# Neighbourhood attention in a diffusion trunk: full-depth score products, a zero-padded half key tile, and a moved value projection

## The chip, the cores and the metric

The kernel runs on one core of one Trainium2 chip. The metric is the device time of one execution in microseconds (us), from three timed runs; lower is better. All arithmetic is in 32-bit floats. Where a product needs accuracy, its operands are split into a high part and a low remainder in a rounded 32-bit format (`F32R`), and two or three products are summed.

## The reference, cut to what matters

The program is one step of a two-layer trunk with 1024 sample tokens (a grid of 16 rows by 64 columns) and 128 prompt tokens. The change lies in the second layer, in mixer C, the neighbourhood attention with 8 heads of 64 channels. Each query reads all 128 context keys and a window of 8 grid rows by 16 columns, in one softmax, with a learned relative bias on the window part:

```
kn = k[:, idx_b];  vn = v[:, idx_b]                  # the 8 x 16 window of each query
s_nb = einsum('bqhd,bqnhd->bhqn', qblk, kn) * scale + rpb[:, dr_b, dc_b]
s_cx = einsum('bqhd,blhd->bhql', qblk, k_ctx) * scale
p = softmax(concatenate([s_cx, s_nb], axis=-1), axis=-1)
out = einsum('bhql,blhd->bqhd', p[..., :L], v_ctx) + einsum('bhqn,bqnhd->bqhd', p[..., L:], vn)
```

The 128 prompt tokens attend among themselves only. q, k, v and a gate come from one input projection of the layer's normalised tokens.

## The kernel before, in words

**Heads in pairs.** `layer1` (L1626) runs four pairs of heads, one `NeighborPair` each. A pair's queries, keys, values and gates are projected channel-major by `Proj.atoms` (L1330): for each of three token groups of 384 columns, eight channel tiles of three products each, into a PSUM bank `cg`. One *atom* is two channel tiles, that is six products of 128x384; one projection is 12 atoms.

**How rows are used.** The pair has 128 channels, 64 per head. `k_split` (L1376) makes for each head h a tile `KH[h]` whose 64 own rows hold the high part of the keys and whose other 64 rows hold a copy of it; ACT writes the high part, DVE subtracts to get the low part, and POOL or DVE copies the high part into the other rows. `q_evac` (L1447) makes `QP[h]`: high part of the scaled queries in head h's rows, low part in the other 64. So one product of 128 rows, `QP[h]` with `KH[h]`, gives high times high plus low times high. The third term, high queries with low keys, is a second product on 64 rows only, with one shared tile `KL` whose rows 0 to 63 belong to head 0 and 64 to 127 to head 1.

**One head, one tile of 128 queries.** `st1` (L1484) makes the scores into two PSUM banks `a`, `b` of a ring of three (tile name `cS`). The queries of tiles 2 to 5 (interior) see 9 grid rows, 576 columns of keys; tiles 0, 1, 6, 7 (edge) see 512; both see 128 context keys; tile 8 is the prompt. The keys are cut in pieces of 512 columns, the 64 left over (interior only) and the 128 of the context; every piece has a full-depth product and a 64-row product (L1506 to L1509). DVE then adds the bias table and takes the running maximum in two instructions (`ttr`, L1517 and L1518) and negates it (`cnm`, L1521); ACT takes the exponential with the row sums (L1522). The bias tables `E` (edge) and `Z` (interior, with 128 zero columns behind) are loaded by `bias` (L1354), masked on POOL by `mask` (L1365). For the edge tiles the context's zeros are the broadcast tile `kn.zero`.

`st2` (L1528) transposes the probabilities on PE in tiles of 128 keys (`cT`) and copies them to `PT` in SBUF, four tiles by ACT, the rest by DVE; the interior's last tile has 64 keys only, so 64 rows. `st3` (L1544) multiplies them with the values for both heads (`cpv`, each head in 64 columns of the array), with 64 rows for the half tile. `norm` (L1555) divides by the sums: `n0` multiplies the gate with `cpv` and takes reciprocals, `n1` spreads them with two half-width products per query tile (`cR`).

**Order.** The order of every engine's queue is written out by hand, as lists of atoms with an assumed cost. `attend` (L1580) lists for the 18 (tile, head) steps n: the scores of n, the transposes of n-2, and on every second step the values of n-4 and n-3. What comes after the last scores is returned apart, as the tail. `weave(main, fill, frac)` (L26) spreads the atoms of `fill` over the first `frac` of `main`; `merge` interleaves two lists. In `layer1` (L1676 to L1703), while pair n attends, the fill is: the last part of its own keys (`last_k`), then the gate, query and value projections of the next pair m, 12 atoms each. After that comes `m.k_start`, and the key projection of m (two token groups, 8 atoms) with the tail of n, the loads and masks of m's bias tables and its SiLU woven in. The fourth pair has as fill `last_k` and two gate projections of the next mixer.

**Memory.** SBUF tiles come from two rings of equal slots, S (25) and W (17). 16 S slots hold the layer's tokens. A weight chunk is loaded (`raw`, SP queue), its high part cast by ACT (`whi`) and its low part subtracted on POOL (`wlo`); `pre` does this for the chunk after the running one.

## Time and profile before

| | |
|---|---|
| three timed runs | 1690.11 us median, 1689.85 to 1690.24 |
| span of the profiled execution, first to last instruction | 1689.1 us; its own time is not recorded apart from this, so the medians' 1.0 us more is what lies around the span |
| instructions | 23950 |
| granted TensorE clock, mean | 0.979 (1.00 in every stretch of the neighbourhood attention) |
| score products of the four pairs, first and last start | 728.2 and 1117.2 us |
| DMA | 105.35 MB, mean 62 GB/s |

In the page, "busy" of PE is the union of modelled, overlapping matmul times, so a busy PE is no sign of a full one: what one product costs is the time from its start to the start of the next. A row of the timeline gives start (us from the span's start), duration (us), engine, line, operation, output<-inputs, array rows*columns and shape (rows x moving columns), count, and in brackets the idle time before it with what ended it. Where line 97 or 106 stands, a helper recorded the instruction, and the tile's name tells the step.

### The profile page before, as it was taken

To read this page: it belongs to the slowest core of one execution; us is meant where nothing else is said; L and a number is where in the kernel's file an instruction comes from. 1 tells how busy PE (TensorE), PEld (TensorE's weight loads), DVE (VectorE), ACT (ScalarE), POOL (GpSimd) and SP (SyncE) were. 2 spreads that over 40 slices of the span, in tenths; PEclk is the share of its full clock that TensorE was granted. 3 is DMA by queue.
4 is the path that set the end of the run, shared out by engine and by line. 5 is a ranking of instruction groups with operands and counts; after the bars stand their busy time and mean duration, and the time that the engine had idled before them with its cause. 6 is when DMAs were issued, how large, how long until landed. Compare 5 with 4: busy or idle time off the path is not lost.

```text
span 1689.1 us, 23950 instructions
## 1 busy us (share of the span) xinstructions
PE 1610.8 (95%) x9268; PEld 1247.9 (74%) x9268; DVE 851.8 (50%) x1839; ACT 647.3 (38%) x1358; POOL 606.3 (36%) x470
## 2 busy tenths in 40 slices
PE   5989999999899999999999999999999999999998
PEld 4968997945554788888888888889975566555686
DVE  3674232467776545524433444324575575766633
ACT  4331211355455323443433434325444343434311
POOL 1642221078567326421310313010135454547421
PEclk7999999999999999999999999999999999999999
DMA  9353013210001222211312113023000000012341
GB/s 305 114 189 88 26 38 131 84 48 14 0 14 50 88 94 73 62 41 34 60 29 51 42 35 58 15 72 96 1 18 19 14 26 14 20 31 82 129 139 50
DMA packets 118806, 105.35 MB, mean 62 GB/s; under 512 B 45924, under 2 KB 104548, under 8 KB 118692
## 3 DMA queue, kind: packets, MB, share of 16 engines
q1 hardware_dynamic: 118692, 103.81, 20.8%
q8 instruction: 73, 1.20, 0.3%
q14 instruction: 41, 0.34, 0.1%
HBM read 88.05 MB, written 15.75 MB: 61 GB/s over the span
## 4 chain that ended last, share of the span: by engine, by line
PE 81%; DVE 7%; ACT 2%; POOL 2%; issue 1%; DMA 0%; SPq 0%; DVEq 0%; POOLq 0%; ACTq 0%
PE cg L97 16%; PE yps L97 10%; PE st L97 9%; PE gate L97 8%; PE pv L97 7%; PE cS L97 6%; PE mp L97 5%; PE lat L97 4%; PE cpv L97 3%; PE cT L106 2%; PE dq L97 2%; PE qkv L97 1%; DVE ms L131 1%; DVE mx L933 1%; PE dk L97 1%
## 5 line engine op out<-in xcount | busy, mean ns | idle before, releaser
L124 POOL TENSOR_TENSOR acc<-acc,P 128x1024 f32<-128x1024 f32 x98 | 233.2, 2380 | 111.1 <-ACT P L969 106.7
L969 ACT ACTIVATE P<-st 128x512 f32<-128x512 f32 x288 | 167.5, 597 | 192.1 <-PE st L97 171.4
L933 DVE TENSOR_REDUCE mx<-mp 128x1 f32<-128x384 f32 x384 | 193.4, 550 | 93.3 <-PE mp L97 90.8
L124 POOL TENSOR_TENSOR wlo<-raw,whi 128x1024 fp32r<-128x1024 f32 x36 | 87.2, 2424 | 270.0 <-ACT whi L113 152.5
L97 PE MATMUL yps<-whi,ohl 128*128 128x512 f32 x576 | 183.4, 393 | 0.0
L97 PE MATMUL cg<-hT1h,whi 128*128 128x384 f32 x480 | 178.0, 371 | 1.8 <-DVE hf L133 1.2
L97 PE MATMUL cg<-hT1h,wlo 128*128 128x384 f32 x480 | 161.8, 337 | 1.8 <-POOL wlo L124 1.8
L97 PE MATMUL cg<-hT1l,whi 128*128 128x384 f32 x480 | 161.6, 337 | 0.0
L97 PEld LDWEIGHTS yps<-whi,ohl 128*128 128x128 f32 x576 | 108.1, 188 | 26.2 <-issue 2.4
L1522 ACT ACTIVATE cs<-cs,cnm 128x640 f32<-128x640 f32 (+1 forms) x64 | 54.9, 857 | 153.3 <-DVE cnm L131 153.0
L97 PE MATMUL yps<-wlo,ohl 128*128 128x512 f32 x288 | 112.2, 389 | 0.0
L97 PE MATMUL gate<-hTh,whi 128*128 128x384 f32 x288 | 100.5, 349 | 5.0 <-ACT whi L113 5.0
L97 PEld LDWEIGHTS cg<-hT1h,whi 128*128 128x128 f32 x480 | 90.3, 188 | 14.5 <-issue 7.0
L97 PE MATMUL gate<-hTh,wlo 128*128 128x384 f32 x288 | 99.2, 344 | 0.9 <-DVE wlo L121 0.9
L97 PE MATMUL gate<-hTl,whi 128*128 128x384 f32 x288 | 98.8, 343 | 0.0
L97 PEld LDWEIGHTS cg<-hT1h,wlo 128*128 128x128 f32 x480 | 90.1, 188 | 2.2 <-POOL wlo L124 2.2
L97 PEld LDWEIGHTS cg<-hT1l,whi 128*128 128x128 f32 x480 | 90.5, 189 | 0.0
L97 PE MATMUL pv<-P,dV 128*64 128x512 f32 x288 | 80.9, 642 | 0.0
L97 PE MATMUL pv<-P,V 128*64 128x512 f32 x288 | 78.6, 624 | 0.0
L113 ACT CAST whi<-raw 128x1024 fp32r<-128x1024 f32 (+2 forms) x60 | 61.8, 1038 | 18.8 <-DMA raw<-in_w_in_o 9.6
L124 POOL TENSOR_TENSOR acc<-P 128x1024 f32<-128x1024 f32 x14 | 33.3, 2380 | 92.9 <-ACT P L969 92.4
L97 PE MATMUL mp<-dKh,QH 96*128 96x384 f32 x192 | 61.2, 374 | 4.1 <-DVE mx L933 2.9
(412 smaller groups left out, 3581.7 us busy)
## 6 DMA issues: line engine op xcount, KB each, us to landing
raw<-in_w_in_o SPq DMA_DIRECT2D x20, 512.0 KB, 4.0
raw<-in_w_in_e SPq DMA_DIRECT2D x18, 512.0 KB, 7.0
wmb<-in_w_mod SPq DMA_DIRECT2D x16, 512.0 KB, 9.0
wm<-in_w_mod SPq DMA_DIRECT2D x16, 512.0 KB, 5.4
wg<-in_w_mod SPq DMA_DIRECT2D x16, 512.0 KB, 3.8
x<-xr SPq DMA_DIRECT2D x9, 512.0 KB, 2.6
xr<-x SPq DMA_DIRECT2D x9, 512.0 KB, 3.9
xn<-in_x_sample SPq DMA_DIRECT2D x8, 512.0 KB, 8.1
```

The costliest lines, as they stand in the source:

```text
L97: self.nc.tensor.matmul(out=out, lhsT=l, rhs=r, start=st, stop=sp)
L106: self.nc.tensor.transpose(out, in_, self.ident[0:n, 0:n])
L113: self.nc.scalar.copy(out=out, in_=in_)
L124: self.nc.gpsimd.tensor_tensor(out=out, in0=a, in1=b, op=op)
L131: self.nc.vector.tensor_scalar(out=out, in0=a, scalar1=s1, scalar2=None, op0=op0)
L933: kn.nc.vector.tensor_reduce(out=self.mx[:, h, t, c:c + 1], in_=b, axis=AX.X, op=ALU.max)
L969: kn.nc.scalar.activation(out=P[:, h], in_=a, func=AF.Exp, scale=self.scale)
L1522: nc.scalar.activation(out=s[:, 0:n], in_=s[:, 0:n], func=AF.Exp, bias=nm, accum_out=sm)
```

## The change

1. **Low keys on 128 rows.** Each head gets its own low-key tiles `KL[h]`, `KLp[h]`; the other head's 64 rows are set to zero once by POOL. They are shared by the four pairs (`NeighborShared`, made at the start of `layer1`). Every score product, high and low, now has 128 rows.
2. **Two key pieces.** The first piece is the 128 context keys together with the first 128 window keys, read as two segments of one access pattern (`seg2`); the second is the rest of the window, 448 columns (interior) or 384 (edge). The scores' columns, the bias tables (128 zero columns now in front, for both tables) and the transposed tiles follow this order; `kn.zero` goes.
3. **Half key tile padded.** The three `PT` buffers are fixed tiles whose slot 5 has zeros in rows 64 to 127, and the values' product of the half tile runs over 128 rows.
4. **Division.** `n0` also has ACT spread the reciprocals to a 128-column tile `crw` (from the W ring), and `n1` uses one full-width product per query tile instead of two half-width ones.
5. **Order.** The value projection of the next pair leaves the fill of the attention and stands ahead of the key projection behind the last scores; `k_start` comes after it; the tail, the bias loads, SiLU and then the masks are spread over the first 0.6 of both. The buffer `kx` is single instead of double.

The program's comments and docstrings were also dropped. The core of the diff:

```diff
+def seg2(x, step):
+    return bass.AP(tensor=x.tensor, offset=x.offset, ap=[list(x.ap[0]), [step, 2], [1, x.shape[1]]])
+
+class NeighborShared:
+    def __init__(self, kn):
+        nc = kn.nc
+        self.KL = [kn.S([128, 1152], F32R, name="cKL") for _ in range(2)]
+        self.KLp = [kn.T([128, 128], F32R, tag=f"cKLp{h}", bufs=1) for h in range(2)]
+        for h in range(2):
+            for x in (self.KL[h], self.KLp[h]):
+                nc.gpsimd.memset(f32(x[64 - 64 * h:128 - 64 * h]), 0.0)
+        self.PT = [kn.T([128, 6, 128], tag=f"PT{i}", bufs=1) for i in range(3)]
+        for x in self.PT:
+            nc.gpsimd.memset(x[64:128, 5, :], 0.0)
...
     def mask(self, h, part):
...
+        nc.gpsimd.memset(T[:, 0:128], 0.0)
         if part:
-            nc.gpsimd.memset(T[:, 576:704], 0.0)
...
     def k_split(self, b, n, KH, KL, pool=False):
...
-            kn.vtt(KL[rs[h]], b[rs[h], 0:n], f32(KH[h][rs[h]]), ALU.subtract)
+            kn.vtt(KL[h][rs[h]], b[rs[h], 0:n], f32(KH[h][rs[h]]), ALU.subtract)
...
     def st1(self, t, h):
...
-        for o, m, src in ((a, 512, k0), (b[:, 0:nk - 512], nk - 512, k0 + 512), (b[:, nk - 512:n - 512], 128, 0)):
-            if m:
-                kn.mm(o, QP[:, q], KH[:, src:src + m], True, False)
-                kn.mm(o, QP[r, q], KL[r, src:src + m], False, True)
+        w0 = 128 + (64 * (row0 - 2 * t + 6) if edge else 0)
+        v2 = lambda x: x.rearrange("p (s c) -> p s c", s=2)
+        for o, x in ((v2(a[:, 0:256]), lambda k: seg2(k[:, 0:128], k0)), (b[:, 0:nk - 128], lambda k: k[:, k0 + 128:k0 + nk])):
+            kn.mm(o, QP[:, q], x(KH), True, False)
+            kn.mm(o, QP[:, q], x(KL), False, True)
...
-        ttr(out=s[:, 0:512], in0=a, in1=T0, scale=1.0, scalar=-3.0e38, op0=ALU.add, op1=ALU.max, accum_out=mx[:, 1:2])
+        ttr(out=v2(s[:, 0:256]), in0=v2(a[:, 0:256]), in1=seg2(T[:, 0:128], w0), scale=1.0, scalar=-3.0e38, op0=ALU.add, op1=ALU.max,
+            accum_out=mx[:, 1:2])
...
     def st2(self, s, tiles):
-        PT = kn.T([128, 6, 128], tag="PT", bufs=3)
+        PT = self.sh.next_PT()
...
     def st3(self, t, PTs, tiles):
...
-                kn.mm(o[64 * h:64 * h + 64, :], v[0:m, 64 * h:64 * h + 64], PTs[h][0:m, i, :], i == 0, i == n - 1)
+                kn.mm(o[64 * h:64 * h + 64, :], v[:, 64 * h:64 * h + 64], PTs[h][:, i, :], i == 0, i == n - 1)
...
     def norm(self, hf):
...
+            w = box["w"] = kn.W([128, 4, 2, 64], name="crw")
+            kn.acopy(w[:, 0:n], r[:, :, 0:n].rearrange("p h t -> p t h")[:, :, :, None].to_broadcast([128, n, 2, 64]))
...
-                for h in range(2):
-                    kn.mm(b[64 * h:64 * h + 64, 128 * t:128 * t + 128], box["r"][:, h, t:t + 1].to_broadcast([128, 64]), kn.ident)
+                kn.mm(b[:, 128 * t:128 * t + 128], box["w"][:, t].rearrange("p h d -> p (h d)"), kn.ident)
...
 def layer1(kn, H, st, fill0):
...
-        fill = last_k + A + [(1, m.q_start)]
-        fill += pre(proj(c + 1).atoms(m.q_evac), c + 1) + pre(m.v_atoms(proj(c + 2)), c + 2)
+        fill = last_k + A + [(1, m.q_start)] + pre(proj(c + 1).atoms(m.q_evac), c + 1)
         fill.insert(-3, (1, m.k_load))
         weave(main, fill, 0.95)
-        m.k_start()
...
-        fill = merge(tab[0] + [(1, lambda: st.need(c + 4))] + tab[1] + [(1, lambda: st._load(c + 5))], tail)
-        fill.insert(-6, (1, m.silu))
-        weave(proj(c + 3).atoms(m.k_evac, (0, 1)), fill, 0.95)
+        fill = merge(tab[0], tail) + [(1, m.silu)] + tab[1]
+        V = pre(m.v_atoms(proj(c + 2)), c + 2)
+        K = proj(c + 3).atoms(m.k_evac, (0, 1))
+        K = [(1, m.k_start)] + K[:3] + [(1, lambda: st.need(c + 4))] + K[3:6] + [(1, lambda: st._load(c + 5))] + K[6:]
+        weave(V + K, fill, 0.6)
```

## The prediction

> **What bounds the kernel now.** I read the page's head first, then a table of stretches over the neighbourhood attention, then who waited there.

> ```profile
> span 1689.1 us, 23950 instructions
> PE 1610.8 (95%) x9268; PEld 1247.9 (74%) x9268; DVE 851.8 (50%) x1839; ACT 647.3 (38%) x1358; POOL 606.3 (36%) x470
> ```

> ```profile
> 936.00:1024.62 88.62, 88.62 (x575) 72.80 (x576) 34.49 (x122) 34.09 (x71) 12.02 (x15) 1.00 0.10 28
> 1040.89:1116.91 76.02, 75.26 (x494) 59.56 (x494) 30.56 (x114) 29.59 (x65) 9.62 (x14) 1.00 0.09 24
> 728.18:1132.57 404.39, 403.40 (x2662) 330.87 (x2661) 153.96 (x539) 163.90 (x334) 67.35 (x64) 1.00 0.18 39
> ```

> ```profile
> PE cS L97 <- DVE cmx L1517: 0.8, 1, 0.8
> ```

> The columns of a stretch are its length, then the busy time (count) of PE, PEld, DVE, ACT and POOL, then the granted clock, here 1.00. The first row runs from the first score of the third pair to its last, the second does so for the fourth, the third covers all four pairs. PE is busy in 403.4 of 404.4 us, DVE and ACT in 154 and 164. The wait row is the whole answer on PE's waits in the same 404 us: one of 0.8 us. So here PE's queue sets the time, and whatever leaves it shortens the kernel, until another engine is late. The second row matters later: the fourth pair has two projections as fill instead of three, the number that the change leaves to the others, and still PE hardly waits.

> **What a score costs PE.** Busy times overlap, so I read starts. First the counts and the reductions, then PE's order around one interior score (851.00) and two value blocks.

> ```profile
> L97 PE MATMUL cS<-cKH,cQP x160: 297/327/502, 728.2 to 1110.2; 128*128 128x512 f32 x64, 128*128 128x128 f32 x64, 128*128 128x64 f32 x32
> L97 PE MATMUL cS<-cKL,cQP x160: 293/324/502, 728.5 to 1110.5; 64*128 64x512 f32 x64, 64*128 64x128 f32 x64, 64*128 64x64 f32 x32
> ...
> L1517 DVE CUSTOM_DVE_ANT_0 cs<-cS,Z x32: 691/692/693, 742.0 to 1089.7; 128x512 f32<-128x512 f32 x32
> L1518 DVE CUSTOM_DVE_ANT_0 cs<-cS,Z,cmx x32: 417/418/420, 743.0 to 1090.7; 128x192 f32<-128x192 f32 x32
> ...
> L97 PE MATMUL cS<-cKLp,cQP x8: 323/324/327, 810.0 to 1117.2; 64*128 64x128 f32 x8
> ```

> ```profile
> 848.59 1.31 PE L97 MATMUL cpv<-PT,cV 128*64 128x128 f32 x20
> 849.84 0.44 PE L97 MATMUL cg<-hT1h,whi 128*128 128x384 f32 x1
> ...
> 851.00 0.39 PE L97 MATMUL cS<-cKH,cQP 128*128 128x512 f32 x1
> 851.32 0.49 PE L97 MATMUL cS<-cKL,cQP 64*128 64x512 f32 x1
> 851.74 0.30 PE L97 MATMUL cS<-cKH,cQP 128*128 128x64 f32 x1
> 851.97 0.29 PE L97 MATMUL cS<-cKL,cQP 64*128 64x64 f32 x1
> 852.19 0.33 PE L97 MATMUL cS<-cKH,cQP 128*128 128x128 f32 x1
> 852.45 0.32 PE L97 MATMUL cS<-cKL,cQP 64*128 64x128 f32 x1
> 852.70 0.44 PE L97 MATMUL cg<-hT1h,whi 128*128 128x384 f32 x1
> 852.99 0.34 PE L97 MATMUL cg<-hT1l,whi 128*128 128x384 f32 x1
> 853.16 0.34 PE L97 MATMUL cg<-hT1h,wlo 128*128 128x384 f32 x1
> ...
> 871.77 1.68 PE L97 MATMUL cpv<-PT,cV 128*64 128x128 f32 x24
> 873.38 0.44 PE L97 MATMUL cg<-hT1h,whi 128*128 128x384 f32 x1
> ```

> For comparison, streams in which every product has the full array, at 256 and at 512 columns:

> ```profile
> 144.66 0.29 PE L97 MATMUL qkv<-whi,hTl 128*128 128x256 f32 x1
> 144.78 0.28 PE L97 MATMUL qkv<-whi,hTh 128*128 128x256 f32 x1
> ```

> ```profile
> 663.47 0.39 PE L97 MATMUL yps<-wlo,ohl 128*128 128x512 f32 x1
> 663.70 0.63 PE L97 MATMUL yps<-whi,ohl 128*128 128x512 f32 x2
> ```

> A full-array product costs 0.12 us for 256 columns, 0.17 for 384 (852.99 to 853.16) and 0.23 for 512; between the last two, 448 columns cost 0.20. The scores cost far more: 64 columns take 0.23 and 0.22, 128 take 0.26, and the 512 of the low keys 0.42. The excess is about 0.2 us per product whatever its length, and it stands wherever the array goes between 128 and 64 rows. Half of it falls on the product before, half on the one after: the first product takes 0.32, and the projection behind the scores still 0.29 instead of 0.17. I take the alternation of row depth as the cause, since `qkv` and `cg` change weights at every product too and pay nothing.

> **The change part by part.**

> Interior score, 32 times (the 64-column form's count): before, 851.00 to 852.70 is 1.70, plus 0.12 on the projection behind, 1.82. After, 2 x 0.12 + 2 x 0.20 = 0.64. Saved 1.18 x 32 = 37.8 us.

> Edge score, 32 times (64 forms of 512 columns less 32): without the two 64-column products, 1.82 - 0.45 = 1.37; after, 2 x 0.12 + 2 x 0.17 = 0.58. Saved 0.79 x 32 = 25.3 us.

> Prompt score, 8 times: one low product between full ones, so two switches of 0.2 less; 3 us, as both streams stay.

> Half value tile: 20 records take 1.25 us, 24 with the half tile 1.61; six fifths of 1.25 are 1.50. Saved 0.11 for each of 16 interior tile pairs (4 tiles x 4 pairs), 1.8 us.

> Division, 12 times (three per pair): same streamed columns, but no change to half-width array and back. From the value block's edge (the same kind of switch) 0.2 to 0.3 each; bounds 0 and 4 us, I take 3. ACT's extra copy lies two score steps ahead of its use, so nobody waits.

> Together 37.8 + 25.3 + 3 + 1.8 + 3 = 71 us off PE.

> The two-segment operand is in no row. Its lower bound is the plain 256-column price, 0.12; its upper bound is that of two plain 128-column products, which at half of the 256's cannot exceed 0.12 each, so 0.12 more on 128 products (2 x 64 scores), 15 us. I take the lower: the row prices show no cost per operand piece, only per column. DVE's two reductions keep their columns: (692 - 418) / 320 = 0.86 ns a column, so 256 and 448 cost as much as 512 and 192, 1.11 us; segments could lengthen that, and DVE at 30.6 of 76 us has room.

> The value projection moves, 12 atoms of six products at 0.17 to 0.18, some 12.6 us per pair for three pairs. PE does it either way, so its cost is zero as long as both places stay full. Behind the scores it is a plain stream and lends cover to the tail. Its other instructions move along: the load of the context values and the store of the prompt's (SP), its evacuations (ACT, DVE), the next chunk's cast and low part (ACT, POOL), all with a dozen atoms of lead. On POOL the masks now precede that `wlo` of the key phase; on SP the bias loads stay first. The single `kx` makes the load of context keys wait for the store of the prompt's, tens of microseconds earlier. The shared `KL` makes the next pair's low keys wait for this pair's last score; twelve value atoms stand between them. I count zero.

> POOL's once-only zeros (two of 64x1152, the rest small) go ahead of this row at the start of the layer:

> ```profile
> 678.81 4.73 POOL L124 TENSOR_TENSOR wlo<-raw,whi 128x1024 fp32r<-128x1024 f32 x2 [6.75 <-ACT whi L113]
> ```

> POOL was idle for 6.75 us before it, more than two clears should take; if they do not fit, PE waits for `wlo` up to 4 us more. I take 0.

> **What is late next.** First the loop of one score: this is ACT's end of it for the score at 851.00.

> ```profile
> 853.62 0.89 ACT L1522 ACTIVATE cs<-cs,cnm 128x704 f32<-128x704 f32 x1 [4.38 <-DVE cnm L131]
> 854.41 0.19 ACT L1522 ACTIVATION_READ_ACCUMULATOR cs<-cs,cnm 128x1 f32 x1
> ```

> The probabilities stand 3.6 us after the score began, and about 0.5 sooner when DVE starts after 0.24 instead of 0.75 us of products. PE wants them two steps later. The fourth pair took 76.0 / 17 = 4.5 us a step; less 0.98 it takes 3.5, so there are 7 us for 3.1. The steady loop keeps up.

> Then the start of a pair, here the fourth:

> ```profile
> 1040.89 0.47 PE L97 MATMUL cS<-cKH,cQP 128*128 128x512 f32 x1
> ...
> 1050.37 0.33 PE L97 MATMUL cS<-cKH,cQP 128*128 128x128 f32 x1 [0.76 <-DVE cmx L1517]
> ```

> ```profile
> 1040.35 2.02 DVE L118 CAST cKH<-cKH 64x384 fp32r<-64x384 f32 x2
> ...
> 1049.61 0.69 DVE L1517 CUSTOM_DVE_ANT_0 cs<-cS,E 128x512 f32<-128x512 f32 x1
> ```

> ```profile
> L118 DVE CAST cKH<-cKH x16: 220/354/2280, 678.8 to 1040.8; 64x128 fp32r<-64x128 f32 x8, 64x384 fp32r<-64x384 f32 x8
> ```

> The fourth score's second bank comes free only with the third score's reduction, which stands on DVE behind key copies and the last keys' low parts, which wait on ACT behind two exponentials. That took 9.5 us from the first score. PE's own work up to there shrinks to three edge scores (1.7), three atoms (3.2), one set of transposes (0.5) and 0.2: 5.6 us. So 3.9 would be missing, less 1.3 if the two copies return from 2.02 us to twice the median of 0.354, as the masks come earlier. I give back 3 us for each of the three pairs with `last_k`, 9 us, bounds 0 and 13.

> Sum: 71 - 9 = 62 saved; 1689.1 - 62 = 1627 of span. The median of the runs is 1.0 above the span, so 1628 us.

> [...] The rows: a `cg` product follows the last by 0.17 us, and its weight load lasts longer than that.

> ```profile
> L97 PEld LDWEIGHTS cg<-hT1h,wlo 128*128 128x128 f32 x480 | 90.1, 188 | 2.2 <-POOL wlo L124 2.2
> ```

> So a load runs under the product before it even though both use all rows. [...]

> **The rivals.**

> No give-back: the pair starts keep up, 1690 - 71 = 1619. For it: the early last-key atoms come sooner as well, so ACT and DVE start sooner. Chance 0.14.

> Dear segments: the two-segment product costs its upper bound, 15 us: 1643. Nothing in the profile speaks for it. 0.10.

> Slack eaten by queues: DVE and ACT serve PE in order, and evacuations and casts between the reductions push the step to about 4.0 us instead of 3.5: 0.5 x 68 steps (17 x 4) = 34 us, 1662. For it: DVE and ACT then work some 30 of 60 us. Against: only one wait in 404 us. 0.10.

> Loads not hidden: each score pays 4 x 0.19 = 0.75 us, 64 of them 48 us: 1676. Against: the `cg` spacing. 0.02.

> The change does not remove the switch: if the 0.2 us belong to the score products as such and not to the row depth, only the two products fewer per interior score count, 0.45 x 32 = 14 us: 1676. Against: the low product of 512 columns costs 0.42 between full-depth ones, `yps` 0.23. 0.03.

> Slower: the loop score, reductions, exponential, transposes becomes the bound outright. With the lag of two it decides from 4.5 us a step, the fourth pair's present pace, where the 62 us are gone; at 4.8 us a step the stage loses 1.3 x 68 = 88 us against 3.5, so 1716. It needs 9.6 us for a chain that shows 3.6. 0.03.

> **How the numbers follow.** The forecast, 1628, has 0.58. Range 1616 to 1655: it takes in the forecast with its bounds, no give-back and dear segments, 0.82 together. 0.2%, 3.4 us, is about what a measurement of this kernel can tell from no change. All cases but the last are faster by more: 0.96 faster; 0.01 same; 0.03 slower.

> **What would show it.** Right: score products only in 128*128 forms of 256, 384 and 448 columns, 0.6 us from the first start to the projection behind; that projection's first product near 0.17 instead of 0.29; a step of 3.5 us; PE's waits in the stage some 10 us, at the third and fourth scores of pairs two to four, named by DVE's reduction. The first step would be wrong if the four products still took over 0.9 us, the second if PE waited over 25 us in the stage for DVE or ACT, the move if PE had gaps in the value and key stretch.

## The result and the profile after

The changed kernel takes 1635.39 us (median of four runs, 1633.59 to 1636.32) against 1690.17 us for the kernel before (four runs, 1689.85 to 1690.57): a ratio of 0.9675, interval 0.9661 to 0.9689. It saves 54.8 us; the forecast was 62, and the time lies inside the range. The profiled execution took 1633.59 us with a span of 1631.8.

The head of the page after, for the two lines shown of before:

```profile
span 1631.8 us, 23732 instructions
PE 1542.5 (95%) x9132; PEld 1232.0 (76%) x9132; DVE 847.1 (52%) x1838; ACT 649.9 (40%) x1370; POOL 610.4 (37%) x485
```

PE's busy time falls by 68 us, the span by 57, and the other engines' busy time hardly moves. The table of stretches after: third pair and fourth pair from first to last score, then the four pairs from the first score to the last division (columns as in the prediction).

```profile
907.64:970.70 63.06, 60.68 (x473) 56.80 (x473) 31.85 (x120) 31.75 (x69) 6.17 (x6) 0.97 0.23 46
999.48:1063.65 64.17, 61.18 (x473) 56.90 (x473) 29.34 (x115) 29.68 (x67) 6.15 (x6) 0.97 0.09 23
728.15:1078.05 349.90, 337.79 (x2527) 316.97 (x2526) 149.62 (x539) 165.97 (x346) 67.67 (x70) 0.99 0.21 45
```

The stage goes from 404.2 to 349.9 us, so the whole gain is here. The third pair's stretch lost 25.6 us, but some 12.6 of that is the value projection, which now stands behind the scores; the fourth pair, which never had it, lost 11.9. Two columns are new: PE is no longer busy throughout (12 us of gaps), and the granted clock in the two pairs is 0.97 where it was 1.00. Who waited in these 350 us, the whole answer for PE:

```profile
PE cS L97 <- DVE cmx L1535: 6.2, 3, 2.1
PE cT L106 <- ACT cs L1541: 1.6, 1, 1.6
PE vT L106 <- ACT vt L113: 1.2, 3, 0.4
PE cpv L97 <- ACT PT L113: 1.0, 2, 0.6
PE cS L97 <- DVE cKH L118: 1.0, 3, 0.3
PE cT L106 <- DVE cQP L127: 1.0, 1, 1.0
```

The columns are total us, times and longest. One short wait has become thirteen, 12.0 us together; half of that is the wait that the prediction named, the score's second bank behind DVE's reduction, three times 2.1 us. The score itself, by its forms and in PE's order, with a value block of another step:

```profile
L97 PE MATMUL cS<-cKH,cQP x128: 277/362/575, 728.2 to 1057.2; 128*128 128x256 f32 x64, 128*128 128x384 f32 x32, 128*128 128x448 f32 x32
...
L97 PE MATMUL cS<-cKL,cQP x128: 278/334/527, 728.3 to 1057.4; 128*128 128x256 f32 x64, 128*128 128x384 f32 x32, 128*128 128x448 f32 x32
...
L1535 DVE CUSTOM_DVE_ANT_0 cs<-cS,Z x32: 405/425/426, 738.1 to 1039.8; 128x256 f32<-128x256 f32 x32
L1537 DVE CUSTOM_DVE_ANT_0 cs<-cS,Z,cmx x32: 683/684/685, 738.7 to 1040.4; 128x448 f32<-128x448 f32 x32
```

```profile
832.83 0.28 PE L97 MATMUL cS<-cKH,cQP 128*128 128x256 f32 x1
832.95 0.28 PE L97 MATMUL cS<-cKL,cQP 128*128 128x256 f32 x1
833.07 0.37 PE L97 MATMUL cS<-cKH,cQP 128*128 128x448 f32 x1
833.28 0.37 PE L97 MATMUL cS<-cKL,cQP 128*128 128x448 f32 x1
833.49 0.34 PE L97 MATMUL cg<-hT1h,whi 128*128 128x384 f32 x1
833.66 0.33 PE L97 MATMUL cg<-hT1l,whi 128*128 128x384 f32 x1
...
845.72 1.53 PE L97 MATMUL cpv<-PT,cV 128*64 128x128 f32 x24
847.18 0.45 PE L97 MATMUL cg<-hT1h,whi 128*128 128x384 f32 x1
```

Read starts: 832.83 to 833.49 is 0.66 us where such a score took 1.70, and the projection behind it 0.17 instead of 0.29. The two-segment products start 0.12 apart, like plain ones of 256 columns. The value block of 24 takes 1.46 us where it took 1.61. DVE's two reductions are 0.425 and 0.684, together 1.11.

Then the wait, in the third pair. First PE, with one stretch behind the wait.

```profile
916.12 0.44 PE L97 MATMUL cS<-cKH,cQP 128*128 128x384 f32 x1 [2.05 <-DVE cmx L1535]
...
916.84 0.53 PE L97 MATMUL cg<-hT1l,whi 128*128 128x384 f32 x1
917.16 0.53 PE L97 MATMUL cg<-hT1h,wlo 128*128 128x384 f32 x1
```

```profile
916.58:920.40 3.82, 3.82 (x16) 3.70 (x16) 2.15 (x11) 2.90 (x6) 0.00 (x0) 0.55 0.00 0
```

The wait costs 2.05 us, and it isn't over when it ends: the next 3.82 us run at a granted clock of 0.55, with projections 0.32 apart instead of 0.17. The fourth pair does the same (1008.42 to 1012.24, 0.55), the second does not (1.00 from 826.42 to 832.67). These two stretches explain the column with 0.97. What DVE and ACT did meanwhile:

```profile
913.54 0.86 DVE L121 TENSOR_TENSOR cKL<-cg,cKH 64x256 fp32r<-64x256 f32 x2 [1.77 <-ACT cKH L113]
915.01 0.59 DVE L121 TENSOR_TENSOR cKLp<-cg,cKHp 64x128 fp32r<-64x128 f32 x2 [0.61 <-ACT cKHp L113]
915.64 0.42 DVE L1535 CUSTOM_DVE_ANT_1 cs<-cS,E 128x256 f32<-128x256 f32 x1
```

```profile
911.81 0.83 ACT L1541 ACTIVATE cs<-cs,cnm 128x640 f32<-128x640 f32 x1 [0.82 <-DVE cnm L131]
...
912.75 0.76 ACT L113 CAST cKH<-cg 64x256 fp32r<-64x256 f32 x2
```

The third score's reduction (915.64) could have begun once its first products were done, around 912. It stands on DVE behind the two low parts of the last keys; those wait for ACT's casts, and the first cast stands behind the second exponential. DVE sits idle for 1.77 and 0.61 us with a ready reduction behind it.

### The profile page after: what moved, and what is told of

The parts are those of the page before. It is cut to its first block, busy times and chain, and to the rows that moved or that the text cites. A ratio compares the mean times of both kernels' runs of the same rounds, so it can differ in the third digit from the quotient of the medians.

```text
span 1631.8 us, 23732 instructions
## 1 busy us (share of the span) xinstructions
PE 1542.5 (95%) x9132; PEld 1232.0 (76%) x9132; DVE 847.1 (52%) x1838; ACT 649.9 (40%) x1370; POOL 610.4 (37%) x485
## 3 DMA queue, kind: packets, MB, share of 16 engines
q8 instruction: 72, 1.18, 0.3%
## 4 chain that ended last, share of the span: by engine, by line
PE 78%; DVE 8%; ACT 3%; POOL 2%; issue 1%; DMA 0%; SPq 0%; DVEq 0%; POOLq 0%; ACTq 0%
PE cg L97 15%; PE yps L97 11%; PE st L97 9%; PE gate L97 8%; PE pv L97 8%; PE mp L97 5%; PE lat L97 4%; PE cpv L97 3%; PE cS L97 2%; PE cT L106 2%; PE dq L97 2%; PE qkv L97 2%; DVE ms L131 1%; DVE mx L933 1%; PE dk L97 1%
## 5 line engine op out<-in xcount | busy, mean ns | idle before, releaser
L124 POOL TENSOR_TENSOR acc<-acc,P 128x1024 f32<-128x1024 f32 x98 | 233.3, 2381 | 109.9 <-ACT P L969 106.3
L124 POOL TENSOR_TENSOR wlo<-raw,whi 128x1024 fp32r<-128x1024 f32 x36 | 87.3, 2427 | 275.6 <-ACT whi L113 220.0
L97 PE MATMUL yps<-whi,ohl 128*128 128x512 f32 x576 | 183.4, 393 | 0.0
L97 PE MATMUL cg<-hT1h,whi 128*128 128x384 f32 x480 | 170.9, 356 | 1.8 <-DVE hf L133 1.2
L97 PE MATMUL cg<-hT1h,wlo 128*128 128x384 f32 x480 | 163.8, 341 | 1.9 <-POOL wlo L124 1.9
L97 PE MATMUL cg<-hT1l,whi 128*128 128x384 f32 x480 | 163.4, 340 | 0.0
L97 PEld LDWEIGHTS yps<-whi,ohl 128*128 128x128 f32 x576 | 108.2, 188 | 26.0 <-issue 2.4
L97 PE MATMUL yps<-wlo,ohl 128*128 128x512 f32 x288 | 112.2, 390 | 0.0
L97 PE MATMUL gate<-hTh,whi 128*128 128x384 f32 x288 | 98.8, 343 | 4.8 <-ACT whi L113 4.8
L97 PE MATMUL gate<-hTh,wlo 128*128 128x384 f32 x288 | 97.5, 339 | 1.3 <-DVE wlo L121 1.3
L97 PE MATMUL gate<-hTl,whi 128*128 128x384 f32 x288 | 97.3, 338 | 0.0
L97 PEld LDWEIGHTS cg<-hT1h,whi 128*128 128x128 f32 x480 | 91.6, 191 | 6.6 <-issue 3.3
L97 PEld LDWEIGHTS cg<-hT1h,wlo 128*128 128x128 f32 x480 | 91.5, 191 | 2.2 <-POOL wlo L124 2.2
L97 PEld LDWEIGHTS cg<-hT1l,whi 128*128 128x128 f32 x480 | 91.7, 191 | 0.5
L1541 ACT ACTIVATE cs<-cs,cnm 128x640 f32<-128x640 f32 (+1 forms) x64 | 54.8, 857 | 92.0 <-DVE cnm L131 91.1
L97 PE MATMUL pv<-P,dV 128*64 128x512 f32 x288 | 80.0, 636 | 0.0
L97 PE MATMUL pv<-P,V 128*64 128x512 f32 x288 | 79.2, 628 | 0.0
L113 ACT CAST whi<-raw 128x1024 fp32r<-128x1024 f32 (+2 forms) x60 | 61.8, 1038 | 22.5 <-DMA raw<-in_w_in_e 8.7
L124 POOL TENSOR_TENSOR acc<-P 128x1024 f32<-128x1024 f32 x14 | 33.4, 2382 | 92.5 <-ACT P L969 91.9
L97 PEld LDWEIGHTS mp<-KH,QP 128*128 128x128 f32 x192 | 33.7, 190 | 41.7 <-DVE mx L933 14.7
```

Source lines behind the costliest of these rows:

```text
L97: self.nc.tensor.matmul(out=out, lhsT=l, rhs=r, start=st, stop=sp)
L113: self.nc.scalar.copy(out=out, in_=in_)
L124: self.nc.gpsimd.tensor_tensor(out=out, in0=a, in1=b, op=op)
L1541: nc.scalar.activation(out=s[:, 0:n], in_=s[:, 0:n], func=AF.Exp, bias=nm, accum_out=sm)
```

## The experiments

The theory: a change of the array's row depth costs about 0.2 us, and the late last keys give part of the gain back at the pair starts. Before's time differed by some us from chip to chip (1686.06 us beside the first four runs, 1686.51 beside the next four, 1686.96 beside the last), so each run is given as a ratio to before on its own chip. "The stage" is the time from the first score product to the last division's last product, in the profiled execution.

**Fewer switches, same products.** On the kernel before, the high products of the first two pieces go first, then their low ones: six switches become four (interior) or four become two (edge); no product changes.

```diff
-for o, m, src in pieces:
-    mm(o, QP, KH, ...); mm(o, QP[r], KL[r], ...)
+for group in (pieces[:2], pieces[2:]):
+    for o, m, src in group: mm(o, QP, KH, ...)
+    for o, m, src in group: mm(o, QP[r], KL[r], ...)
```

> The kernel before, with the same six (edge: four) score products in another order: the high products of the first two pieces, then their low products on 64 rows; in an interior score the context piece follows as before. Changes of row depth per score fall from 6 to 4 (interior) and from 4 to 2 (edge). Theory of the prediction (0.2 us per change of row depth): 2 x 0.2 us x 64 scores = 26 us less, about 1665 us, and a low product that follows a low product costs its columns alone. Rival (a product on 64 rows is dear in itself, or every small piece is): no change, 1690 us.

Measured: 1673.15 us, ratio 0.9920 (0.9902 to 0.9939), stage 385.0. One interior score in PE's order:

```profile
857.93 0.43 PE L97 MATMUL cS<-cKH,cQP 128*128 128x512 f32 x2
858.29 0.53 PE L97 MATMUL cS<-cKL,cQP 64*128 64x512 f32 x2
858.74 0.33 PE L97 MATMUL cS<-cKH,cQP 128*128 128x128 f32 x1
859.00 0.32 PE L97 MATMUL cS<-cKL,cQP 64*128 64x128 f32 x1
859.25 0.44 PE L97 MATMUL cg<-hT1h,whi 128*128 128x384 f32 x1
```

The rows show shape and count of a group of products; the first two hold 512 and 64 columns each. The score takes 1.32 us instead of 1.70, and the low 512 and 64 together 0.45, where they took 0.42 and 0.22 apart. So here a 64-row product was not dear in itself; the changes of depth were: two fewer took 0.38 us off the score, 0.19 each. The stage is 19.2 us shorter. With the excess of single blocks taken out, as explained under the give-back below, PE's own work shrank by 24.4 us, against 26 expected, and 5.3 of that came back: waits at the three fourth scores (4.0 us together, longest 2.0, where before had one of 0.8), and 3.4 us at half clock behind the longest. So the give-back appears as soon as PE gets faster, without the rest of the change. The time fell by less than the stage, 12.9 us of 1686.06, half of what was expected. Outside the stage, where the kernels do the same work, executions differ by some us: the first score stands at 731.2 us, in before's profile at 728.2, and the mean granted clock of the whole execution is 0.975, there 0.979. So for what happens in the stage its own length says more than the time.

**The move alone.** The new order of value and key projection, on the kernel before.

```diff
-fill += pre(proj(c + 1)...) + pre(m.v_atoms(proj(c + 2)), c + 2)
+fill += pre(proj(c + 1)...)
...
-weave(proj(c + 3).atoms(m.k_evac, (0, 1)), fill, 0.95)
+weave(V + K, fill, 0.6)
```

> The kernel before with the new order alone: value projection ahead of the key projection behind the last scores, the tail, bias loads, SiLU and masks spread over 0.6 of both. Theory: PE does the same work and keeps full, 1690 us, at most 3 us more from the starts of the second and third pair, which then wait as the fourth does (0.8 us). Rival (the move itself brings part of the gain, or costs by gaps in the value and key stretch): over 5 us either way.

Measured: 1691.57 us, ratio 1.0033 (1.0019 to 1.0047), stage 407.3. PE's waits, the whole answer:

```profile
PE cS L97 <- DVE cmx L1517: 2.3, 3, 0.8
PE cS L97 <- DVE cKH L118: 1.7, 3, 0.6
PE vT L106 <- ACT vt L113: 0.8, 3, 0.3
```

The move by itself loses: 4.8 us of waits where before had 0.8, among them the first score of a pair behind DVE's copies of the keys, which now finish last. Why it was made can only be argued from the code: a second `KL` tile would be a 26th slot in the S ring of 25 while the next pair's value tile is made during the attention.

**128 rows alone.** The previous run with low keys on 128 rows, but the old pieces (512, 64, 128), half tile and division.

```diff
-kn.mm(o, QP[r, q], KL[r, src:src + m], False, True)
+kn.mm(o, QP[:, q], KL[h][:, src:src + m], False, True)
```

> New order and low keys on 128 rows with the zeroed halves; key pieces of 512, 64 and 128 columns, half value tile and division as before. Theory: an interior score costs 2 x (0.23 + 0.11 + 0.11) = 0.90 us of PE, an edge score 0.68, so PE loses 0.92 x 32 + 0.69 x 32 + 3 = 55 us, and waits at the pair starts give back some 14: 1649 us. Rival (the two pieces are what saves): 1680 us or more.

Measured: 1648.96 us, ratio 0.9784 (0.9765 to 0.9803), stage 366.6, that is 42.6 us less time and 40.7 us less stage than the move alone; the wait at the fourth scores grows to three times 2.5 us. The forecast of 1649 was made from before's 1690; beside this run before took 1686.06, so 37 us were saved where 41 were expected.

**64 rows again.** The changed kernel with only the low products back on 64 rows.

```diff
-kn.mm(o, QP[:, q], x(KL), False, True)
+kn.mm(o, QP[r, q], x(KL[r]), False, True)
```

> The changed kernel with the low products back on 64 rows (two key pieces, padded half tile, division and order as changed). Theory: four changes of row depth per score come back, 0.8 us x 64 + 0.4 x 8 = 54 us of PE; the waits at the pair starts (some 18 us in the changed kernel) shrink under it by about 10: 1635 + 44 = 1679 us. Rival (two pieces and order carry the gain): at most 1650 us.

Measured: 1673.28 us, ratio 0.9921 (0.9895 to 0.9946), stage 389.2.

```profile
849.72 0.36 PE L97 MATMUL cS<-cKH,cQP 128*128 128x256 f32 x1
850.02 0.38 PE L97 MATMUL cS<-cKL,cQP 64*128 64x256 f32 x1
850.33 0.47 PE L97 MATMUL cS<-cKH,cQP 128*128 128x448 f32 x1
850.72 0.47 PE L97 MATMUL cS<-cKL,cQP 64*128 64x448 f32 x1
851.12 0.45 PE L97 MATMUL cg<-hT1h,whi 128*128 128x384 f32 x1
```

The same four products over the same columns take 1.40 us when every second one uses 64 rows; the changed kernel takes 0.72 for a score that stands behind transposes like this one (1018.59 to 1019.31). The zero rows are worth about 40 us of stage in either direction (40.7 added to the move, 39.3 taken from the changed kernel); pieces, half tile and division together make the other 16.7 us of stage between the run before this one and the changed kernel. PE's waits fall from 12.0 to 3.9 us here and the half clock is gone; by the same sums as below, PE's own work grew by some 52 us, against 54 expected, and 13 of that was hidden by the shorter give-back.

**The same kernel again**, beside the next three runs.

> The changed kernel again, as a control on the same chip for the three runs beside it: 1635 us.

Measured: 1633.13 us, ratio 0.9692 (0.9666 to 0.9718). Its profiled execution ran at a mean granted clock of 0.926 instead of 0.979, so only its time is used.

**Last keys later.** The last part of the keys is taken up behind three gate atoms instead of before the first.

```diff
-fill = last_k + A + ...
+fill = A[:4] + last_k + A[4:] + ...
```

> The changed kernel with one edit: the last two atoms of a pair's own key projection stand behind the first three atoms of the gate projection in the fill, so that their splits on ACT and DVE come after the first scores' reductions and not between the second and the third. Theory (the wait of 2.3 us at the fourth score of pairs two to four is DVE's queue held by the last keys' low parts, which wait for ACT): it goes, and the waits behind it; 3 x (2.3 + 1) = 7 to 10 us less, 1626 us. Rival (the first scores are bound by DVE's reductions or the score banks whatever stands between them): under 2 us.

Measured: 1644.34 us, ratio 0.9754 (0.9736 to 0.9771), stage 361.7: slower than the changed kernel, a miss. The first row of PE's waits, and a stretch behind the last of them:

```profile
PE kpT L106 <- ACT vt L113: 13.2, 3, 4.4
```

```profile
1020.00:1027.00 7.00, 6.66 (x36) 5.99 (x37) 0.38 (x2) 1.59 (x5) 0.00 (x0) 0.53 0.34 87
```

The wait at the fourth score is gone from the answer, as the theory has it. But the store of the prompt's keys now stood directly behind the late keys: its transposes (`kpT`) waited 4.4 us in each of three pairs, and half-clock stretches of 6.8 us followed. I had moved the producer and left its consumer where it was.

**Later, and the copies on POOL.** The previous run, with the second key group's copies on POOL instead of DVE.

```diff
-self.k_split(..., g != 1)
+self.k_split(..., True)
```

> As the run with later last keys, and the copies of the second key group into the other head's rows on POOL instead of DVE. Theory: the first score of pairs two to four, now 0.5 us late for DVE's copy, comes on time, and DVE's first reduction 0.7 us sooner: 1 to 2 us less than the run beside it, 1625 us. Rival (POOL's copy is slower and is itself what is waited for): no gain or 1 us more.

Measured: 1642.03 us, ratio 0.9732 (0.9714 to 0.9749), stage 357.6. The waits at the first scores (1.0 us together in the previous run) are gone, so DVE's copies did cause them; the `kpT` waits stay at 13.2 us. In time the gain on the previous run isn't resolved (the intervals overlap), and part of the 4.1 us of stage is half clock: two of its three stretches are 3.4 us long instead of 6.8.

**The old division** in the changed kernel:

```diff
-kn.mm(b[...], box["w"][:, t]..., kn.ident)
+for h in range(2):
+    kn.mm(b[64 * h:64 * h + 64, ...], box["r"][:, h, t:t + 1]..., kn.ident)
```

> The changed kernel with the old division: two half-width products per query tile, no spreading copy on ACT. Prediction's term: 3 us more, bounds 0 and 4: 1638 us. Rival (the copy on ACT makes PE wait at the last division of a pair, 0.65 us three times, and the full-width products cost as much): no more than 1 us either way.

Measured: 1636.37 us, ratio 0.9708 (0.9687 to 0.9728), which overlaps the same kernel's 0.9692 beside it: the times don't resolve it. The stage, 352.5 us, is 2.6 longer, with other waits in it: those at the fourth scores are 7.3 us instead of 6.2, others shorter. The wait behind a pair's last division, which the rival puts down to the spreading copy, stays without it: 0.3 us three times instead of 0.4, each time for ACT's copy of the values (`vT` behind `vt`).

**Keys and store later.** The changed kernel with last keys behind three gate atoms and the key store six list entries further on.

```diff
-A.insert(4, (110, n.k_out))
-fill = last_k + A + ...
+A.insert(10, (110, n.k_out))
+fill = A[:4] + last_k + A[4:] + ...
```

> The changed kernel with a pair's last key atoms behind three gate atoms, as in the run with later last keys, and the transposes of the prompt's keys for their store six atoms later still, so that PE does not stand at them for ACT's copy. In the run with later last keys the wait at the fourth score was gone, but PE waited 4.4 us at those transposes in each of three pairs. Theory: both waits are gone, 3 x (2.3 + about 1 behind it) less than the changed kernel, 1626 to 1628 us. Rival (the wait only moves on to the next consumer of the same late splits, or to DVE's reductions): no less than 1632 us.

Measured: 1628.29 us, ratio 0.9656 (0.9643 to 0.9669), stage 342.7. The first row of PE's waits, and the stage:

```profile
PE cg L97 <- DVE PT L118: 2.1, 3, 0.7
```

```profile
727.74:1070.42 342.68, 334.60 (x2526) 313.23 (x2526) 149.79 (x539) 165.84 (x346) 67.55 (x70) 1.00 0.21 46
```

The stage is 7.2 us shorter than after: no row names the fourth scores' second bank any more, 6.2 us there became the 2.1 of the first row, and the clock is 1.00 throughout, which returns the 3.3 us of the two half-clock stretches (4.1 + 3.3 = 7.4). This confirms where that part of the give-back came from. The time alone doesn't resolve it: the interval overlaps that of the changed kernel (0.9661 to 0.9689), and by the ratios the gain is 3 us; that the time meets the forecast of 1626 to 1628 is in part this chip, where before took 1686.96 us.

**The copies on POOL as well.** The previous run with `k_split(..., True)`.

> The run beside it, and the copies of the second key group on POOL instead of DVE: the first score of pairs two to four comes 0.5 us sooner; 1 to 2 us less, 1625 us. Rival: nothing that can be measured.

Measured: 1625.63 us, ratio 0.9639 (0.9626 to 0.9653). The interval lies below that of the changed kernel (0.9661 to 0.9689), so this version beats both kernels. Against the previous run (0.9643 to 0.9669) it isn't resolved, and its stage, 342.9 us, is no shorter: the first scores' waits are gone, but in the first pair a wait of 1.4 us and one of 0.4 lie close together, and this follows:

```profile
766.00:770.00 4.00, 3.58 (x26) 3.25 (x27) 1.10 (x5) 2.61 (x5) 2.36 (x1) 0.57 0.00 0
```

**First scores further apart.** The previous run, with more fill between the first three scores of each pair.

```diff
-L.append((1000, lambda n=n: s(n)))
+L.append((1600 if n < 3 else 1000, lambda n=n: s(n)))
```

> The run with POOL copies, and the first three scores of a pair entered with a cost of 1600 instead of 1000, so that more of the fill stands between them and less later. Theory: the first pair's wait of 1.7 us at its third score is three reductions of 1.5 us on DVE against 1.6 us of PE work a score, and shrinks; 1 to 2 us less, 1623 us. Rival (the fill is then short later): no gain or a loss.

Measured: 1629.39 us, ratio 0.9663 (0.9647 to 0.9679), stage 345.9: 3 us of stage longer instead of shorter, a miss; the times overlap. The first pair's wait for the exponential fell from 1.6 to 0.6 us, but new waits came in three places each, as the rival has it: transposes behind DVE's copies of the probabilities (4.5 us together) and behind its query evacuation (3.2, where the previous run had 1.4).

**The half tile on 64 rows** in the changed kernel:

```diff
-kn.mm(o[...], v[:, 64 * h:64 * h + 64], PTs[h][:, i, :], ...)
+kn.mm(o[...], v[0:m, 64 * h:64 * h + 64], PTs[h][0:m, i, :], ...)
```

> The changed kernel with the values' product of the half key tile on 64 rows again. Prediction's term: 0.11 us in each of 16 value blocks, 1.8 us more, 1637 us; a value block of 24 records takes 1.61 us instead of 1.46. Rival: nothing, since it is within what a run can tell.

Measured: 1636.9 us, ratio 0.9705 (0.9690 to 0.9721), stage 353.8.

```profile
753.49 1.68 PE L97 MATMUL cpv<-PT,cV 128*64 128x128 f32 x24
755.09 0.44 PE L97 MATMUL cg<-hT1h,whi 128*128 128x384 f32 x1
```

The block is back at 1.60 us from 1.46, 2.4 us over 16 blocks with what lies around them. The rest of the stage's 3.9 us is a third half-clock stretch: here all three pairs have one behind the fourth score's wait.

## Why the prediction was right, and where it was short

**Scores: right.** Forecast 66 us from interior, edge and prompt scores. Summed from start to start over the stage, with waits and the other excess that is listed under the give-back taken out, the score products fell from 101.0 to 44.0 us. The first projection product behind a score lost its excess too (0.28 us before, 0.17 after), 6.9 us together: 63.9. The mechanism, a price per change of row depth, is shown by grouping alone (two switches fewer, same products: 1.32 us for 1.70) and by the zero rows from both sides (40.7 and 39.3 us of stage). The rival that the change doesn't remove the switch falls with it, and so does the one with loads not hidden: full-depth products of 256 columns start 0.12 us apart here, under loads of 188 ns.

**Segments: right.** 0.12 us between the two-segment products, no more than plain; DVE's reductions 1.11 us as worked out.

**Half tile and division: right in size.** Forecast 1.8 and 3 us. By the same sums the value blocks fell by 3.2 us (2.4 by the run on 64 rows). The division's products fell by 2.2 and the projection products ahead of them by 1.1 (0.27 us before, 0.17 after): 3.3. Neither is resolved by the times alone. Two things I had not counted: the transposes took 1.4 us more, since seventeen of their blocks run straight into a value block instead of nine, which costs 0.17 each; and the projections fell by another 2.5 where they border on other blocks, mostly because they stand beside a value block less often.

**Gain on PE: right.** All together PE's own work fell by 71.4 us (54.3 of stage and 17.1 of net give-back, below), forecast 71; the terms above give 63.9 + 3.2 + 3.3 - 1.4 + 2.5 = 71.5. In the part for the scores 2 us are missing, and the borders, which were in no term, made up for it; so the closeness of the sum is in part luck.

**Give-back: right in place, too small in size.** The failed step is the term of 9 us, 3 per pair, with its companion "The steady loop keeps up": I counted waits at one place per pair and nothing elsewhere. Measured as the excess of each block of PE's products over the median of its kind, the give-back is 18.7 us after and 1.6 before (the fourth pair's fourth score and the first scores of three pairs), 17.1 net:

- Fourth scores, the place forecast: 2.33 us in each of three pairs, 7.0. With 3.3 for the two half-clock stretches behind them 10.3, against 9; the half clock was no part of the forecast.
- First scores of pairs two to four, behind DVE's key copies: 1.5. I had let the copies come back to their short time, and they did (0.74 for two instead of 2.02); they still end after PE arrives.
- Where there are no late keys at all: 1.75 in the first pair, where the first transposes come before the first exponential has ended, and 2.4 at its first division (767 to 772 us), where the gate's product and ACT's copies of the probabilities stand behind a query evacuation.
- 1.0 in the last pair, at a value block, and 1.7 behind the last divisions of the first three pairs. There the last transposes of the moved value projection wait for ACT's copy (`vT` behind ACT's `vt` in the list of waits), which the prediction had put at nothing with "a dozen atoms of lead": the copy for the last token group has none.

So 17.1 came back instead of 9. That is 8.1 more, against the 7.2 by which the saving fell short of the forecast (62 less 54.8); PE's own work came out 0.4 larger, and the times differ by 0.5 more than the stages. The steady loop between these places does keep up: no other block of the stage is more than 0.25 us over the median of its kind, and a step of the third pair takes 63.06 / 17 = 3.71 us, less 0.26 for its own 4.4 us of give-back (17 steps) 3.45, where 3.5 were forecast. So the statement failed at starts and ends of pairs and at one division, not in the loop, and the rival that queues eat the slack in every step falls too. The move was counted at zero, and it isn't: alone it costs 3.1 us of stage, and the waits at the first scores of pairs two to four (1.7 us) and behind the last divisions (0.8 us) appear with it, before anything else is changed. POOL's zeros cost nothing: its seven clears took 3.0 us together (669.3 to 672.2 us), and the first score starts at 728.15 us, before at 728.18.

**Left open.** The spot at 767 to 772 us, the last pair's 1.0 us and the waits behind the last divisions weren't tried by themselves. That the moved value projection was needed for the memory is argued from the code only.

## What to carry to other kernels

Price a matmul from its start to the next start, and look for the price of what alternates: the same four products cost 0.72 us or 1.40 us a score here, depending only on whether all used the same rows. Where a second operand needs fewer rows, zero rows can be cheaper than a change of depth, as they were here by some 40 us of stage. When PE's work shrinks, look for the give-back at the starts of stages, where other engines' queues hold late work in front of what PE needs; move that work together with its consumer, and look behind a PE wait of 2 us for more: here two of three cost 1.6 us more each, in the stretch at half clock behind them.

## What the runs showed of the hardware that was not expected

A wait of about 2 us on PE was often followed by 3.4 us at half clock. After the 2.05 us waits of the changed kernel it stood in two of three pairs (0.55 over 3.82 us each, 1.6 us lost each time), after waits of up to 2.5 us in the run with 128 rows alone in two of three as well, and with the half tile on 64 rows in all three; behind the 4.4 us waits for `kpT` it lasted 6.8 us in the run with the last keys later. In the stage of before, and of the runs with waits of 1.6 us at most (the move alone, low keys on 64 rows, keys and store later, first scores apart), there was none; with 1.4 and 0.4 us close together there was one.

```profile
824.48:827.89 3.41, 1.92 (x12) 1.88 (x13) 2.66 (x11) 1.57 (x6) 0.58 (x2) 1.00 0.00 0
913.23:916.64 3.41, 1.36 (x11) 1.16 (x10) 2.28 (x7) 1.07 (x4) 1.33 (x4) 1.00 0.00 0
916.64:920.05 3.41, 3.41 (x15) 3.32 (x14) 1.96 (x10) 2.83 (x6) 0.00 (x0) 0.50 0.00 0
```

In the third pair the whole wait lies in one window (3.41 less 1.36 is 2.05 us without PE), and the next window runs at 0.50. In the second pair a wait of the same length is cut by the grid, the larger part is 1.49 us, and the next window runs at 1.00. Over the stage of these traces, all 16 full-clock windows with 1.96 us or more of such gaps were followed by half clock, and of those with 1.75 us or less only one was, with 1.60 us, in the run with the copies on POOL as well. So here two waits of equal length cost different amounts, 2.05 us and 2.05 with 1.6 behind it, by where they fell on the grid.

Outside the stage a smaller gap stood before it too: before's window from 1253.83 to 1257.24 us has 1.30 us without PE, and the next one runs at 0.50. No run changed a wait's length alone, so that the wait causes the half clock is an inference from these places.

DVE's two key copies of 64x384 took 2.02 us before (from 1040.35 us), while POOL was masking (1.53 us for one mask from 1040.47), and 0.74 in the changed order (from 907.86 us), where POOL stood idle beside them. That POOL's work slows the copies is an inference from this overlap.
